# Modulation sums: block transposes and sums by 32 on VectorE ahead of a 128x32 selection matmul, in place of a column sum on TensorE

## The chip, the cores and the metric

One core of one Trainium2 chip. The metric is device time of one execution in microseconds (us); lower is better. The profile is of a single execution, so its own time is given beside the median of the timed runs.

## The reference

Two layers of a decoder trunk on 256 tokens of width 1024, all in float32. Each layer has three sublayers (a SwiGLU feed-forward, a mixer, a SwiGLU feed-forward); the mixer is forgetting attention ("fox") in the first layer and HGRN2 in the second. Around each sublayer stands the same conditioning, from one vector c for the whole sequence:

```python
cond = silu(c)                                              # (1, 1024)
for i in range(2):
    mod = (cond @ ada_w[i] + ada_b[i]).reshape(1, 3, 3, 1, 1024)
    h = rms_norm(x, norm_g[i, s]) * (1 + mod[:, s, 1]) + mod[:, s, 0]
    x = x + gate_factor * mod[:, s, 2] * sublayer(h)        # s = 0, 1, 2
```

So there are 6 sublayers with 3 modulation vectors each (shift, scale, gate), every one of them a product of a 1024-vector with a 1024x1024 matrix `ada_w`. This study is about how the last step of these products is done.

## The kernel before

**The main work.** Activations lie transposed, 128 features by 256 tokens in a tile, 8 tiles. Every weight matrix is streamed from HBM in float32 pieces of 128x1024 (`raw`, 8 buffers). ScalarE rounds a piece to a high part `wh` (line 371), VectorE takes the rest as `wl` (line 372), and TensorE makes each product in three passes (`mm3`, lines 728 to 730): high by high, high by low, low by high. The three buffers of `wh` and `wl` let the split run two weight items ahead of the item that TensorE reads (`SPLIT_AHEAD`). An item of an up-projection is 16 calls of `mm3`.

**The order of the work.** The program is written out as one sequence. `plan` lists the weight items of all sublayers in order and puts the `ada` items (one 128x1024 piece of `ada_w` each) between them, at most of the time of the sublayer before the one that needs them. After each `mm3` the method `tick` counts a clock `now` up by one; it calls `pump`, which emits at most one step of the split (a piece of a main item or one `ada` item), and it advances side tasks. A side task is a generator: it emits some instructions and yields the number of ticks until it is to be advanced again. So one tick is three matmuls of TensorE's queue, and a yield of n puts what follows n `mm3` calls later into the program. A scheduler of the language then sets each engine's instruction order from this sequence and from what is ready in its own model of the time; the engines run their queues in order.

**The modulation, part by part.** For all vectors but the first sublayer's shift and scale, 16 in number (these are called parts here), `ada_step` (line 405) takes the 8 pieces k = 0..7 of the matrix one at a time on VectorE: k = 0 writes `adaacc` = raw times the scalar `cond[:, k]` (line 410), the others add to it (line 412). `adaacc` is 128x1024 and has one buffer: the next part's line 410 must wait until the last reader of the present part is done. After k = 7 the vector is the sum of `adaacc` over its 128 partitions. `ada_finish` (line 459), an urgent side task that is first advanced in the tick of k = 7, makes that sum:

- it waits `SUM_LAG` = 30 ticks;
- line 465: four float32 matmuls, each with a 128x32 block of ones as weights and a strided quarter of `adaacc` (256 columns) as the moving operand. Quarter j writes PSUM partitions 32j to 32j+31, so the four lie in four column groups of the array. All 32 rows of a group hold the same sums. The profile shows each as two records, 8 in all for a part;
- 4 ticks later, line 469: VectorE transposes the 128x256 result in 32x32 blocks from PSUM, which puts the 1024 sums into 8 columns of 128 partitions;
- line 471: VectorE adds the bias `adab`, reading every 32nd column; `set_mods` (line 480) then forms the final vector.

The constants (identity, causal mask, selections) come with one small DMA into `cst` at the start.

Of the kernel before, what the change touches and what calls it, by code (L numbers as in the profile page):

```python
# [11 lines left out]
F32 = mybir.dt.float32  # L12
# [4 lines left out]
ALU = mybir.AluOpType  # L17
AX = mybir.AxisListType

P = 128  # L20
S = 256
D = 1024
# [9 lines left out]

RAW_BUFS = 8
SPLIT_AHEAD = 2
SUM_LAG = 30
FOLD = (5, 4)
H_LAG = 0
HEAD = 7
# [20 lines left out]
def shape_constants():  # L59
    i = np.arange(P)  # L60
    ident = np.eye(P, dtype=np.float32)
    causal = np.where(i[None, :] > i[:, None], np.float32(NEG), np.float32(0)).astype(np.float32)
    lcross = (i[:, None] > i[None, :]).astype(np.float32)
    masks = np.zeros((P, len(LEV), P), np.int32)
    for li, b in enumerate(LEV):
        masks[:, li] = i[:, None] // b == i[None, :] // b
    sel4 = np.zeros((P, 4), np.float32)
    sel1 = np.zeros((P, 1), np.float32)
    for j in range(4):
        sel4[32 * j, j] = 1  # L70
        sel1[32 * j, 0] = 1
    selq = np.zeros((P, 16), np.float32)
    for h in range(16):
        selq[h, h] = -1
        selq[64 + h, h] = -1
    consts = np.concatenate([ident, causal, sel4, selq, sel1], axis=1)
    return (np.ascontiguousarray(consts), np.ascontiguousarray(lcross),
            np.ascontiguousarray(masks.reshape(P, -1)))

# [13 lines left out]
class Trunk:  # L93
# [364 lines left out]

    def ada_finish(self, l, s, part, total):
        nc = self.nc  # L460
        yield SUM_LAG
        ps = self.bank("adaps")
        quarters = total.rearrange("p (c j w) -> p j c w", j=4, w=32)
        for j in range(4):
            nc.tensor.matmul(ps[32 * j:32 * j + 32, :S], self.ones[:, :32], quarters[:, j],  # L465
                             start=True, stop=True, skip_group_check=True)
        yield 4
        tr = self.wk.tile([P, S], F32, tag="adatr", name="adatr", bufs=1)
        nc.vector.transpose(tr, ps[:, :S])
        mod = self.wk.tile([P, 8], F32, tag=f"mod{part}", name=f"mod{l}{s}{part}", bufs=3)  # L470
        nc.vector.tensor_tensor(mod, tr.rearrange("p (c i) -> p c i", i=32)[:, :, 0],
                                self.adab[:, l * 72 + (s * 3 + part) * 8:][:, :8], ALU.add)
        self.set_mods(l, s, part, mod)

    def mod(self, l, s, what):
# [19 lines left out]
    def setup(self):  # L495
        nc, cp, a = self.nc, self.cp, self.a
# [5 lines left out]
        rows = big[:80, 7552:7680]  # L502
        crow = big[:8, 7680:7808]
        self.ident = cp.tile([P, P], F32, name="ident")
        cst = cp.tile([P, 149], F32, name="cst")
        warm = self.w("warm")
        nc.gpsimd.memset(warm[:, 0:1], 0.0)
        nc.scalar.activation(warm[:, 1:2], warm[:, 0:1], AF.Silu)
# [20 lines left out]
            small = small[2:]  # L529
        self.ones = cp.tile([P, P], F32, name="ones")  # L530
        nc.vector.memset(self.ones, 1.0)
        self.sel4 = cst[:, 128:132]
        self.selq = cst[:, 132:148]
        self.sel1 = cst[:, 148:149]
        self.mhalf = cp.tile([P, 2], F32, name="mhalf")
        nc.gpsimd.memset(self.mhalf, -0.5)
        self.tm = cp.tile([P, P], F32R, name="tm")
# [38 lines left out]
        l, s = divmod(self.subs[0], NSUB)  # L576
# [695 lines left out]
def build(inputs, subs=(0, 1, 2, 3, 4, 5), final=True):  # L1272
    nc = bacc.Bacc("TRN2", target_bir_lowering=False, num_devices=1)
    arrays, args = {}, {}
    consts, tmat, lmask = shape_constants()
    every = {n: np.ascontiguousarray(inputs[n]) for n in _INS}
    every["x"] = flip(every["x"])
    every.update(consts=consts, tmat=tmat, lmask=lmask)
    for name, arr in every.items():
        arrays[f"in_{name}_dram"] = arr  # L1280
        args[name] = nc.dram_tensor(f"in_{name}_dram", arr.shape, mybir.dt.from_np(arr.dtype),
                                    kind="ExternalInput").ap()
    out = nc.dram_tensor("out_0_dram", (1, S, D), F32, kind="ExternalOutput").ap()
    with tile.TileContext(nc) as tc:
        with ExitStack() as ctx:
            Trunk(ctx, tc, args, out, list(subs), final).run()
    return nc, arrays
# [6 lines left out]
```

## Time and profile before

| | us |
|---|---|
| median of 3 timed runs | 1105.64 (1105.61 to 1108.42) |
| the profiled execution | 1107.98 |
| its span, first to last instruction | 1106.1 |
| TensorE busy | 1084.1 |
| VectorE busy | 838.7 |
| ScalarE busy | 587.9 |

The mean granted TensorE clock of the profiled execution is 0.995 of full speed. In the profile PE is TensorE's matmul, PEld its weight load, DVE is VectorE, ACT ScalarE, POOL GpSimd, SP SyncE; L465 is line 465 of the kernel. An instruction's recorded duration includes latency that overlaps its neighbour's, so the distance from one start to the next is the better price of one in a full queue. A row of a timeline has start, duration, engine, line, operation, output and inputs, shape and count; the bracket holds the idle time of the engine before it and what ended that.

### The profile page before, as it was taken

Reading aid. Unit: us, or ns where it says so; the run is one execution under the profiler, and the core shown is the slowest. Engines: PE = TensorE matmul, PEld = TensorE weight load, DVE = VectorE, ACT = ScalarE, POOL = GpSimd, SP = SyncE. Lnnn points to the kernel's source line nnn. Section 1 sums busy time; section 2 is a strip of 40 time slices with the busy share of each in tenths; the row PEclk is TensorE's granted clock in tenths of the full one; section 3 lists DMA queues with packets and bytes.
Section 4 is the critical chain, followed back from the end, with each engine's and each line's share of the span. In section 5 each row is a group of like instructions: output and inputs, shape, how many; then the busy total and the mean of one; then the engine's idle time right before and its main releaser. Section 6 shows DMA issues by size and latency. Waiting matters only on the chain.

```text
span 1106.1 us, 22061 instructions
## 1 busy us (share of the span) xinstructions
PE 1084.1 (98%) x8835; PEld 1055.6 (95%) x8835; DVE 838.7 (76%) x1486; ACT 587.9 (53%) x1105; POOL 23.1 (2%) x46
## 2 busy tenths in 40 slices
PE   6999999999999999999999999999999999999997
PEld 6999999988999999999999999999998999999997
DVE  6987789587996797888579888777987879555542
ACT  5454444376865664444355444445777756444443
POOL 0000000020000000000000000000000000000000
PEclk9999999999999999999999999999999999999999
DMA  9999998759974579998958999995643456665530
GB/s 300 334 316 316 323 330 266 213 168 328 298 236 137 162 221 313 312 320 307 259 173 252 286 335 320 322 294 172 191 145 117 122 157 190 188 189 173 179 109 39
DMA packets 304707, 260.24 MB, mean 235 GB/s; under 512 B 9525, under 2 KB 281501, under 8 KB 304605
## 3 DMA queue, kind: packets, MB, share of 16 engines
q1 hardware_dynamic: 304172, 257.79, 76.0%
q8 instruction: 69, 1.13, 0.4%
q0 software_dynamic: 288, 0.52, 0.2%
q10 hardware_dynamic: 144, 0.52, 0.1%
q14 instruction: 34, 0.27, 0.1%
HBM read 257.75 MB, written 1.05 MB: 234 GB/s over the span
## 4 chain that ended last, share of the span: by engine, by line
PE 76%; issue 18%; ACT 3%; POOL 1%; DMA 1%; DVE 1%; SPq 0%; POOLq 0%; DVEq 0%; ACTq 0%
PE pf L729 17%; PE pf L728 16%; PE pf L730 16%; PE pd L728 6%; PE pd L729 6%; PE pd L730 6%; PE pA L1172 1%; ACT wh L371 1%; PE pv L881 1%; PE pv L879 1%; PE pv L880 1%; PE adaps L465 1%; PE sc L998 1%; DMA raw<-in_ffn_w_up_dram 1%; PE pt L1020 1%
## 5 line engine op out<-in xcount | busy, mean ns | idle before, releaser
L729 PE MATMUL pf<-hbuf,wh 128*128 128x256 f32 (+1 forms) x1920 | 543.8, 284 | 0.9 <-DVE hbuf L589 0.9
L730 PE MATMUL pf<-hbuf,wl 128*128 128x256 f32 (+1 forms) x1920 | 543.2, 284 | 0.0
L728 PE MATMUL pf<-hbuf,wh 128*128 128x256 f32 (+1 forms) x1920 | 539.0, 284 | 0.6 <-ACT hbuf L588 0.6
L371 ACT CAST wh<-raw 128x1024 fp32r<-128x1024 f32 x338 | 341.6, 1027 | 370.1 <-PE pf L729 219.0
L372 DVE TENSOR_TENSOR wl<-raw,wh 128x1024 fp32r<-128x1024 f32 x338 | 400.2, 1194 | 158.3 <-ACT wh L371 157.1
L728 PEld LDWEIGHTS pf<-hbuf,wh 128*128 128x128 f32 x1920 | 363.4, 191 | 4.8 <-issue 4.0
L729 PEld LDWEIGHTS pf<-hbuf,wh 128*128 128x128 f32 x1920 | 365.1, 190 | 1.2 <-DVE hbuf L589 1.1
L730 PEld LDWEIGHTS pf<-hbuf,wl 128*128 128x128 f32 x1920 | 364.6, 190 | 0.8 <-issue 0.8
L728 PE MATMUL pd<-gx,wh 128*128 128x256 f32 x704 | 197.5, 281 | 0.0
L729 PE MATMUL pd<-gx,wh 128*128 128x256 f32 x704 | 196.7, 279 | 0.0
L730 PE MATMUL pd<-gx,wl 128*128 128x256 f32 x704 | 196.4, 279 | 0.0
L412 DVE SCALAR_TENSOR_TENSOR adaacc<-raw,cond,adaacc 128x1024 f32<-128x1024 f32 x112 | 142.9, 1276 | 0.9 <-DMA raw<-in_ada_w_dram 0.4
L728 PEld LDWEIGHTS pd<-gx,wh 128*128 128x128 f32 x704 | 132.3, 188 | 2.5 <-issue 2.5
L730 PEld LDWEIGHTS pd<-gx,wl 128*128 128x128 f32 x704 | 132.3, 188 | 0.0
L729 PEld LDWEIGHTS pd<-gx,wh 128*128 128x128 f32 x704 | 132.3, 188 | 0.0
L794 ACT CAST gx<-g 128x256 fp32r<-128x256 f32 x88 | 35.6, 406 | 25.8 <-DVE g L836 18.3
L796 DVE TENSOR_TENSOR gx<-g,gx 128x256 fp32r<-128x256 f32 x88 | 36.6, 418 | 0.2
L410 DVE TENSOR_SCALAR adaacc<-raw,cond 128x1024 f32<-128x1024 f32 x16 | 12.1, 756 | 25.4 <-PE adaps L465 25.4
L836 DVE TENSOR_TENSOR g<-sa,pf 128x256 f32<-128x256 f32 x73 | 30.1, 414 | 0.4 <-ACT sa L835 0.2
L801 DVE SCALAR_TENSOR_TENSOR x<-pd,mod,x 128x256 f32<-128x256 f32 x32 | 14.3, 479 | 20.5 <-PE pd L730 20.5
L835 ACT ACTIVATE sa<-pf 128x256 f32<-128x256 f32 x73 | 27.4, 377 | 0.0
L360 ACT CAST wh<-raw 128x896 fp32r<-128x896 f32 x16 | 15.0, 935 | 23.0 <-DMA raw<-in_ffn_w_up_dram 23.0
(218 smaller groups left out, 859.2 us busy)
## 6 DMA issues: line engine op xcount, KB each, us to landing
raw<-in_ffn_w_up_dram SPq DMA_DIRECT2D x162, 512.0 KB, 5.5
raw<-in_ada_w_dram SPq DMA_DIRECT2D x128, 512.0 KB, 5.8
raw<-in_ffn_w_down_dram SPq DMA_DIRECT2D x76, 512.0 KB, 5.7
raw<-in_fox_w_in_dram SPq DMA_DIRECT2D x32, 512.0 KB, 5.3
raw<-in_hgrn_w_in_dram SPq DMA_DIRECT2D x32, 512.0 KB, 4.5
raw<-in_ada_w_dram SPq DMA_DIRECT2D x32, 256.0 KB, 6.9
raw<-in_ffn_w_up_dram SPq DMA_DIRECT2D x16, 448.0 KB, 6.6
raw<-in_fox_w_out_dram SPq DMA_DIRECT2D x8, 512.0 KB, 5.1
```

Source lines behind the costliest of these rows:

```text
L360: nc.scalar.copy(wh[:, k, cs], raw)
L371: nc.scalar.copy(wh[:, ks, cs], raw)
L372: nc.vector.tensor_tensor(wl[:, ks, cs], raw, wh[:, ks, cs].bitcast(F32), ALU.subtract)
L412: nc.vector.scalar_tensor_tensor(self.ada_acc, raw, self.cond[:, k:k + 1], self.ada_acc, ALU.mult, ALU.add)
L728: nc.tensor.matmul(ps, wh, hx[:, :n], start=first, stop=False, skip_group_check=True)
L729: nc.tensor.matmul(ps, wh, hx[:, lo:lo + n], start=False, stop=False, skip_group_check=True)
L730: nc.tensor.matmul(ps, wl, hx[:, :n], start=False, stop=last, skip_group_check=True)
L794: nc.scalar.copy(dst[:, :S], v)
L796: nc.vector.tensor_tensor(dst[:, lo:lo + S], v, dst[:, :S].bitcast(F32), ALU.subtract)
L801: nc.vector.scalar_tensor_tensor(self.x[:, m, :], ps, gate[:, m:m + 1], self.x[:, m, :], ALU.mult, ALU.add)
L835: nc.scalar.activation(sa, ps[0], AF.Silu)
L836: nc.vector.tensor_tensor(g, sa, ps[1], ALU.mult)
```

## The change

The sum over partitions is split. First VectorE transposes `adaacc` in 32x32 blocks, four chunks of 256 columns, and sums each group of 32 columns of the transposed chunk; the result `red` is 128x32 and holds, at partition 32a+i and column b, the sum of the 32 values of `adaacc` in partitions 32a to 32a+31 at column 32b+i. What is left is to add the four partitions i, 32+i, 64+i, 96+i. TensorE does this with a 128x32 selection matrix `sel32` as weights and 8 columns of `red` as moving operand, four times, into the same four groups of PSUM partitions. The result is in its final place, so the transpose from PSUM falls away and the bias add reads PSUM.

```diff
-SUM_LAG = 30
+SUM_LAG = 8
...
+    sel32 = (i[:, None] % 32 == np.arange(32)[None, :]).astype(np.float32)
...
     def ada_finish(self, l, s, part, total):
         nc = self.nc
+        red = self.wk.tile([P, 32], F32, tag="adared", name="adared", bufs=1)
+        for o in range(0, D, S):
+            tr = self.wk.tile([P, S], F32, tag="adatr", name="adatr", bufs=1)
+            nc.vector.transpose(tr, total[:, o:o + S])
+            nc.vector.tensor_reduce(red[:, o // 32:(o + S) // 32], tr.rearrange("p (b j) -> p b j", j=32), AX.X, ALU.add)
+            yield 3
         yield SUM_LAG
         ps = self.bank("adaps")
-        quarters = total.rearrange("p (c j w) -> p j c w", j=4, w=32)
+        quarters = red.rearrange("p (c j) -> p j c", j=4)
         for j in range(4):
-            nc.tensor.matmul(ps[32 * j:32 * j + 32, :S], self.ones[:, :32], quarters[:, j],
+            nc.tensor.matmul(ps[32 * j:32 * j + 32, :8], self.sel32, quarters[:, j],
                              start=True, stop=True, skip_group_check=True)
         yield 4
-        tr = self.wk.tile([P, S], F32, tag="adatr", name="adatr", bufs=1)
-        nc.vector.transpose(tr, ps[:, :S])
         mod = self.wk.tile([P, 8], F32, tag=f"mod{part}", name=f"mod{l}{s}{part}", bufs=3)
-        nc.vector.tensor_tensor(mod, tr.rearrange("p (c i) -> p c i", i=32)[:, :, 0],
-                                self.adab[:, l * 72 + (s * 3 + part) * 8:][:, :8], ALU.add)
+        nc.vector.tensor_tensor(mod, ps[:, :8], self.adab[:, l * 72 + (s * 3 + part) * 8:][:, :8], ALU.add)
         self.set_mods(l, s, part, mod)
...
-        cst = cp.tile([P, 149], F32, name="cst")
+        cst = cp.tile([P, 176], F32, name="cst")
```

The matmuls of a part thus come 4 x 3 + 8 = 20 ticks after k = 7 instead of 30. Two unused selection constants are dropped, and `cst` grows from 149 to 176 columns.

More of the change, by code (lines that the diff above doesn't have):

```diff
@@ L66, in shape_constants @@
         masks[:, li] = i[:, None] // b == i[None, :] // b
[L67 to L71, printed above, removed]
+    sel32 = (i[:, None] % 32 == np.arange(32)[None, :]).astype(np.float32)
     selq = np.zeros((P, 16), np.float32)
@@ L75, in shape_constants @@
         selq[64 + h, h] = -1
-    consts = np.concatenate([ident, causal, sel4, selq, sel1], axis=1)
+    consts = np.concatenate([ident, causal, selq, sel32], axis=1)
     return (np.ascontiguousarray(consts), np.ascontiguousarray(lcross),
@@ L531, in setup @@
         nc.vector.memset(self.ones, 1.0)
-        self.sel4 = cst[:, 128:132]
-        self.selq = cst[:, 132:148]
-        self.sel1 = cst[:, 148:149]
+        self.selq = cst[:, 128:144]
+        self.sel32 = cst[:, 144:176]
         self.mhalf = cp.tile([P, 2], F32, name="mhalf")
```

## The prediction

> **What bounds the kernel now.** I read the page first: busy shares and the chain that ended last.
>
> ```profile
> span 1106.1 us, 22061 instructions
> PE 1084.1 (98%) x8835; PEld 1055.6 (95%) x8835; DVE 838.7 (76%) x1486; ACT 587.9 (53%) x1105; POOL 23.1 (2%) x46
> ...
> PE pf L729 17%; PE pf L728 16%; PE pf L730 16%; PE pd L728 6%; PE pd L729 6%; PE pd L730 6%; PE pA L1172 1%; ACT wh L371 1%; PE pv L881 1%; PE pv L879 1%; PE pv L880 1%; PE adaps L465 1%; PE sc L998 1%; DMA raw<-in_ffn_w_up_dram 1%; PE pt L1020 1%
> ```
>
> TensorE is busy for 98% of the span, and the chain is made of its matmuls. The step that the change rewrites, L465, is in that chain with about 1%. A busy PE needn't be a full one, so I looked at what TensorE waited for:
>
> ```profile
> PE pv L546 <- DMA ident<-in_consts_dram: 3.2, 1, 3.2
> PE pr L563 <- DMA cst<-in_consts_dram: 2.8, 1, 2.8
> PE rb L688 <- DVE diag L687: 1.8, 3, 1.2
> ```
>
> The columns are total, times, longest. The longest waits are once each, at the start; behind it no wait of its matmuls costs more than 2 us in all. So TensorE's queue is the clock of this kernel: a microsecond taken out of that queue comes off the time, as long as no other engine is late for it. The two questions are how long the 16 sums occupy TensorE, and whether VectorE keeps up.
>
> **TensorE's part.** The timeline of TensorE around the first sum, then its weight loads in the same stretch:
>
> ```profile
> 105.33 0.27 PE L728 MATMUL pf<-hbuf,wh 128*128 128x256 f32 x1
> 105.44 0.28 PE L729 MATMUL pf<-hbuf,wh 128*128 128x256 f32 x1
> 105.56 0.28 PE L730 MATMUL pf<-hbuf,wl 128*128 128x256 f32 x1
> 105.77 0.64 PE L465 MATMUL adaps<-adaacc,ones 128*32 128x256 f32 x8
> 106.34 0.38 PE L728 MATMUL pf<-hbuf,wh 128*128 128x256 f32 x1
> 106.56 0.28 PE L729 MATMUL pf<-hbuf,wh 128*128 128x256 f32 x1
> 106.68 0.29 PE L730 MATMUL pf<-hbuf,wl 128*128 128x256 f32 x1
> ```
>
> ```profile
> 105.45 0.19 PEld L730 LDWEIGHTS pf<-hbuf,wl 128*128 128x128 f32 x1
> 105.77 0.16 PEld L465 LDWEIGHTS adaps<-adaacc,ones 128*32 128x32 f32 x8
> 106.34 0.19 PEld L728 LDWEIGHTS pf<-hbuf,wh 128*128 128x128 f32 x1 [0.41 <-issue]
> ```
>
> Ordinary matmuls start every 0.12 us. Around the sum the starts are 0.21, 0.57 and 0.22 us apart; two ordinary steps would have taken 0.24 of these 1.00 us, so one part takes 0.76 us out of the stream, and 16 parts take 12.2 us: the whole prize if the sum cost TensorE nothing.
>
> The 0.57 us are streaming, and that goes. The rows of this tile give the duration of one record and the count:
>
> ```profile
> L465 PEld LDWEIGHTS adaps<-adaacc,ones x128: 106/108/110, 105.8 to 736.6; 128*32 128x32 f32 x128
> L465 PE MATMUL adaps<-adaacc,ones x128: 379/391/404, 105.8 to 736.8; 128*32 128x256 f32 x128
> L469 DVE STREAM_TRANSPOSE adatr<-adaps x16: 440/443/450, 107.2 to 738.2; 128x256 f32<-128x256 f32 x16
> ...
>   DVE adaacc L410: 25.4, 11
> ```
>
> 128 records are 8 for each of 16 parts. Eight records of 391 ns within 640 ns are two waves of four, one record for each column group; the second wave starts about 0.64 - 0.38 = 0.26 us in. With 8 columns instead of 256 the streaming is next to nothing, and what is left is the fixed price of eight small float32 matmuls. The trace of before has no matmul with 32 columns of weights and few moving columns. Two rows bound it. From above, the sums of the first sublayer, with one moving column but weights of 128 columns:
>
> ```profile
> 28.86 0.95 PE L448 MATMUL adac<-ones,adc 128*128 128x1 f32 x8
> 29.67 0.37 PE L728 MATMUL pf<-hbuf,wh 128*128 128x256 f32 x1
> ```
>
> Eight of them hold the queue for 0.81 us, 0.10 each, although they stream nothing: their weight loads set the pace. At that price a part would be 0.24 us dearer than now, +3.8 us for 16. From below: the eight loads of 128x32 in L465 last 108 ns each and all eight fit into 0.16 us, so they start some 7 ns apart; at that pace eight small matmuls take 0.06 us, and with another 0.1 us until the next ordinary load (an estimate by the first step, which is 0.21 - 0.12 = 0.09 too long) they leave 0.16 of the 0.57 us: 0.41 x 16 = 6.6 us saved. I take the loads as proportional to their columns: 0.10 us / 4 = 0.025 us each, 0.20 us for eight. It lies near the lower row because the change keeps exactly that 128x32 load. So 0.57 becomes 0.20 us, and 16 x 0.37 = 5.9 us leave TensorE's queue.
>
> The 0.09 us by which the first step is over 0.12 us, and the 0.10 us of the last, I leave in place: the new matmuls are 32 columns wide too. If they went, 16 x 0.19 = 3.0 us more would be saved; that is outside my range. The Trainium skill has a rule for it (TensorEngine Tiling (Array Packing), Key Properties): changing the tiling mode drains TensorE. The trace agrees, as the steps into and out of the 32-wide matmuls are 0.21 and 0.22 us long, and by the rule 3.0 us stay.
>
> **VectorE's part.** Added for each part are four block transposes of 128x256 and four sums of 128x256; removed is one transpose. The nearest row of a sum is the maximum over 256 columns, beside an elementwise product of that size:
>
> ```profile
> L1004 DVE TENSOR_REDUCE nm<-sc 128x1 f32<-128x256 f32 x16 | 6.6, 414 | 0.0
> L836 DVE TENSOR_TENSOR g<-sa,pf 128x256 f32<-128x256 f32 x73 | 30.1, 414 | 0.4 <-ACT sa L835 0.2
> ```
>
> By recorded durations 4 x 443 + 4 x 414 - 443 = 2.99 us for a part, 48 us in all. Now the timeline of VectorE from k = 7 of the first part to the start of the next part:
>
> ```profile
> 93.39 1.28 DVE L412 SCALAR_TENSOR_TENSOR adaacc<-raw,cond,adaacc 128x1024 f32<-128x1024 f32 x1
> 95.86 1.23 DVE L372 TENSOR_TENSOR wl<-raw,wh 128x1024 fp32r<-128x1024 f32 x1 [1.19 <-ACT wh L371]
> 97.00 0.41 DVE L836 TENSOR_TENSOR g<-sa,pf 128x256 f32<-128x256 f32 x1
> 97.34 1.22 DVE L372 TENSOR_TENSOR wl<-raw,wh 128x1024 fp32r<-128x1024 f32 x1
> 98.47 0.42 DVE L796 TENSOR_TENSOR gx<-g,gx 128x256 fp32r<-128x256 f32 x1
> 101.56 1.23 DVE L372 TENSOR_TENSOR wl<-raw,wh 128x1024 fp32r<-128x1024 f32 x1 [2.67 <-ACT wh L371]
> ...
> 103.03 1.22 DVE L372 TENSOR_TENSOR wl<-raw,wh 128x1024 fp32r<-128x1024 f32 x1
> 104.16 0.42 DVE L796 TENSOR_TENSOR gx<-g,gx 128x256 fp32r<-128x256 f32 x1
> 106.48 0.75 DVE L410 TENSOR_SCALAR adaacc<-raw,cond 128x1024 f32<-128x1024 f32 x1 [1.90 <-PE adaps L465]
> 107.15 0.44 DVE L469 STREAM_TRANSPOSE adatr<-adaps 128x256 f32<-128x256 f32 x1
> 107.52 1.24 DVE L412 SCALAR_TENSOR_TENSOR adaacc<-raw,cond,adaacc 128x1024 f32<-128x1024 f32 x1
> ```
>
> By starts a transpose takes 0.37 us (107.15 to 107.52) and a 256-column operation 0.34 (97.00 to 97.34), so the eight take 2.8 us, net 2.5 us a part, 39 us in all. Against that stands the wait of L410 for L465, 25.4 us over 11 parts: `adaacc` is now free as soon as VectorE itself has read it. Where the new work goes is seen above: k = 7 ends at 94.67, then VectorE idles 1.19 us, later 2.67 and 1.90 us. 5.8 us of holes hold 2.8 us of work.
>
> Does this make `wl` late? ScalarE's splits show the beat of the main items:
>
> ```profile
> 94.78 1.05 ACT L371 CAST wh<-raw 128x1024 fp32r<-128x1024 f32 x1 [3.12 <-PE pf L729]
> 100.47 1.05 ACT L371 CAST wh<-raw 128x1024 fp32r<-128x1024 f32 x1 [2.61 <-PE pf L729]
> ```
>
> One item takes 5.7 us, and an item is split two items ahead. The split that begins at 100.47 has its second `wl` done at 104.2; TensorE needs it at 100.5 + 11.4 = 111.9. Some 7.6 us of lead cover a burst of 2.8 us. Were that lead gone, each part would cost TensorE up to 2.5 us. ScalarE, the DMA queue on SP and POOL get no new instruction; the earlier freedom of `adaacc` frees `raw` buffers earlier, so loads start no later. The 27 extra columns of `cst` go with a transfer that is there already; I price them at nothing. So I do the bias add of 8 columns, which only reads another place, and the one buffer of `red`: TensorE has read it 20 ticks behind k = 7, and the next part needs it some 30 us later.
>
> Does the new wait bite? TensorE's L465 now waits for the last sum. At 0.36 us a tick (three starts 0.12 apart) the matmuls stood 30 ticks or 10.7 us behind k = 7 in the program, and now 20 ticks or 7.2 us. k = 7 ended 11.1 us ahead of L465, so VectorE is 0.4 us early and has until 94.67 + 7.6 = 102.3. If only one pair (0.7 us) fits into the first hole and the other three (2.1 us) stand behind L796, the last sum is done at 98.8 + 2.1 = 100.9. That leaves 1.4 us. Behind a late sum stand all main matmuls.
>
> The tightest stretch is the attention stage, with three of the 16 sums. Its windows, beside one of a feed-forward:
>
> ```profile
> 276.00:305.00 29.00, 28.92 (x230) 26.57 (x226) 26.51 (x55) 23.17 (x63) 0.00 (x0) 1.00 0.88 289
> 305.00:339.00 34.00, 33.93 (x272) 30.01 (x271) 29.85 (x57) 23.27 (x60) 0.00 (x0) 1.00 0.78 247
> 621.00:651.00 30.00, 30.00 (x261) 29.12 (x259) 24.48 (x31) 13.95 (x21) 0.00 (x0) 1.00 0.97 292
> ```
>
> The third busy column is VectorE. With 2.5 us more the feed-forward window is at 27.0 of 30, the first attention window at 29.0 of 29. There the queue will be full and some of attention's own steps late; I allow 0.5 us of loss, from nothing to 2.5 us for each of the three, 7.5 us.
>
> **Sum.** 5.9 us saved, 0.5 lost: 5.4 us. The profiled execution took 1107.98 us (its span and 1.9 us around it), so it would take 1102.6; it lay 2.3 us above the median of the three timed runs, so against 1105.64 the forecast is 1100.2.
>
> **Rivals.**
>
> *The sum is late for TensorE (slower).* If one more `wl` of the next item comes ahead of the last pair, with its wait for ScalarE, the last sum ends at 101.56 + 1.15 + 0.7 = 103.4 instead of 100.9, 1.1 us after TensorE needs it. In all 16 parts that is 17.6 - 5.9 = 11.7 us slower, 1117.3; it decides once the average lateness is over 0.37 us. For it: the cover shrinks by a third. Against: all four pairs are written within 9 ticks of k = 7, in the first part ahead of the next item's split, and need nothing but VectorE. Chance 0.07.
>
> *The weight loads set the price (slower).* At L448's 0.81 us: +3.8 us, 1109.4. Against: 32-column loads are seen 7 ns apart. Chance 0.04.
>
> *VectorE is full in attention (no change).* If the three parts there cost 2 us each, 6 us eat the gain: 1105.7. The Trainium skill speaks against the change here (VectorE: DVE Perf Modes, Rules for kernel authors): it calls tensor_reduce the slowest operation of that engine and advises restructuring on a hot path. At this size the trace doesn't agree, 414 ns against 414 for a product, so I don't raise the chance: 0.15, along with smaller losses elsewhere.
>
> **The numbers.** The forecast case has 0.74. 0.3% (3.3 us) is about what a measurement of this kernel can tell from no change. Faster by more has the forecast case's 0.74; within it the third rival and half of the weight-load one, 0.17; slower the rest, 0.09. The forecast's own ends are 1099.0 (6.6 saved, none lost) and 1102.3. The range of 8 in 10 goes a little beneath the first, for the 3.0 us of drain, and above to 1104.5, most of the third rival.
>
> **What would show it.** Right: L465 x8 followed by the next L728 after about 0.2 us instead of 0.57; no wait of L410 for L465; VectorE busy some 39 us more; no new wait of L465 for the sum; the windows of the feed-forward shorter by 0.37 us for each sum. Wrong: L465 still above 0.4 us, a wait PE adaps <- DVE adared of more than a few tenths each, or idle time ahead of attention's matmuls.

## The result, and the profile after

| | before | after |
|---|---|---|
| median of the timed runs, us | 1105.79 | 1097.39 |
| their range, us | 1104.51 to 1108.42 | 1097.2 to 1099.45 |
| profiled execution, us | 1107.98 | 1097.96 |
| its span, us | 1106.1 | 1096.2 |

The ratio is 0.9923, with a 95% interval of 0.9911 to 0.9935: 8.4 us faster. The prediction was 1100.2, and its range began a little beneath 1099.0. The direction was right; the time lies under the range, 1.6 us below that 1099.0 and 2.8 us under the forecast.

The page after, first the span and the busy times, then the two new groups of VectorE:

```profile
span 1096.2 us, 22151 instructions
...
PE 1072.4 (98%) x8835; PEld 1049.2 (96%) x8835; DVE 883.3 (81%) x1598; ACT 586.7 (54%) x1105; POOL 23.1 (2%) x46
...
L460 DVE STREAM_TRANSPOSE adatr<-adaacc 128x256 f32<-128x256 f32 x64 | 28.3, 442 | 1.4
L461 DVE TENSOR_REDUCE adared<-adatr 128x8 f32<-128x256 f32 x64 | 26.7, 418 | 1.6
```

TensorE is still busy for 98% and is 11.7 us shorter in busy time; VectorE has 44.6 us more. The timeline of TensorE around the first sum, as the prediction showed it for before:

```profile
99.84 0.28 PE L727 MATMUL pf<-hbuf,wh 128*128 128x256 f32 x1
99.96 0.28 PE L728 MATMUL pf<-hbuf,wl 128*128 128x256 f32 x1
100.17 0.25 PE L467 MATMUL adaps<-adared,cst 128*32 128x8 f32 x8
100.35 0.38 PE L726 MATMUL pf<-hbuf,wh 128*128 128x256 f32 x1
100.57 0.28 PE L727 MATMUL pf<-hbuf,wh 128*128 128x256 f32 x1
```

The starts around the sum are 0.21, 0.18 and 0.22 us apart, 0.61 where two ordinary steps take 0.24. A part takes 0.37 us out of the stream instead of 0.76. The first and the last step are as they were; the middle one fell from 0.57 to 0.18 us.

The waits that bear on the change (total, times, longest, in us), those of VectorE and then those of TensorE:

```profile
DVE adaacc L408 <- DMA raw<-in_ada_w_dram: 16.5, 17, 3.5
...
PE pd L728 <- DVE wl L368: 1.1, 2, 0.7
...
PE adaps L467 <- DVE adared L461: 0.2, 1, 0.2
```

The wait of the first `adaacc` step for the sum, 25.4 us before, is gone. VectorE now runs ahead until it meets the loads of `ada_w` instead (16.5 us). The new wait of the sum for VectorE's last step is there once, 0.2 us. The wait of a main matmul for `wl` lies in the second down-projection: there VectorE stands in `adaacc` behind a load, with a `wl` queued behind it.

**Where the time went in the two traces.** I added up, over all of TensorE's matmuls, by how much each step from one start to the next is longer than 119.3 ns, the mean step of the up-projections in the trace of before. The spans differ by 9.9 us. The sums give 6.1 of it (16 parts: 12.1 us of excess before, 6.0 after). 2.9 us lie in two stretches in which before was at half clock and after wasn't; they are taken up in the last section. The second down-projection lost 1.7 us to the waits above (0.5 in a second profile of the changed kernel). What was not on the list of the prediction is a closer spacing of the ordinary matmuls in the first and the fourth down-projection, 1.7 and 1.0 us. A stretch of 20 us of the first down-projection, free of sums, shows it. The first column after the stretch and its length is PE, busy time and number of matmuls; the number includes two or three that straddle the edges. Before:

```profile
171.00:191.00 20.00, 20.00 (x174) 20.00 (x173) 19.96 (x25) 9.54 (x13) 0.00 (x0) 1.00 0.90 286
```

After:

```profile
168.00:188.00 20.00, 20.00 (x179) 20.00 (x178) 19.45 (x28) 10.11 (x14) 0.00 (x0) 1.00 1.06 322
```

TensorE is busy all of the time at full clock in both, waits for nothing, and still passes five matmuls more. From their starts the step is 116.7 ns before and 113.3 after. The busy share can't show this.

### The profile page after: what moved, and what is told of

Read it like the earlier page. It is cut to its first block, busy times and chain, and to the rows that moved or that the text cites. A ratio compares the mean times of both kernels' runs of the same rounds, so it can differ in the third digit from the quotient of the medians.

```text
span 1096.2 us, 22151 instructions
## 1 busy us (share of the span) xinstructions
PE 1072.4 (98%) x8835; PEld 1049.2 (96%) x8835; DVE 883.3 (81%) x1598; ACT 586.7 (54%) x1105; POOL 23.1 (2%) x46
## 4 chain that ended last, share of the span: by engine, by line
PE 62%; issue 19%; DVE 9%; DMA 5%; ACT 3%; POOL 1%; SPq 0%; POOLq 0%; DVEq 0%; ACTq 0%
PE pf L727 13%; PE pf L726 13%; PE pf L728 13%; PE pd L726 5%; PE pd L728 5%; PE pd L727 5%; DMA raw<-in_ada_w_dram 5%; DVE wl L368 3%; DVE adaacc L408 2%; ACT wh L367 1%; PE pA L1170 1%; PE pv L879 1%; PE pv L877 1%; PE pv L878 1%; PE sc L996 1%
## 5 line engine op out<-in xcount | busy, mean ns | idle before, releaser
L408 DVE SCALAR_TENSOR_TENSOR adaacc<-raw,cond,adaacc 128x1024 f32<-128x1024 f32 x112 | 143.4, 1280 | 17.5 <-DMA raw<-in_ada_w_dram 16.5
L460 DVE STREAM_TRANSPOSE adatr<-adaacc 128x256 f32<-128x256 f32 x64 | 28.3, 442 | 1.4
L461 DVE TENSOR_REDUCE adared<-adatr 128x8 f32<-128x256 f32 x64 | 26.7, 418 | 1.6
```

Of the source, the lines that this page charges most:

```text
L408: nc.vector.scalar_tensor_tensor(self.ada_acc, raw, self.cond[:, k:k + 1], self.ada_acc, ALU.mult, ALU.add)
L460: nc.vector.transpose(tr, total[:, o:o + S])
L461: nc.vector.tensor_reduce(red[:, o // 32:(o + S) // 32], tr.rearrange("p (b j) -> p b j", j=32), AX.X, ALU.add)
```

## The experiments

The theory on entering them: the sums' occupancy of TensorE is the gain, and VectorE's work is hidden. The rivals: the earlier place of the sum or the free `adaacc` brings the gain; VectorE's work costs something; and, later, something other than the sum sets the spacing.

### Is it the earlier sum, or VectorE's work?

**before_lag8** puts the old sum at 8 ticks instead of 30:

```diff
-SUM_LAG = 30
+SUM_LAG = 8
```

> The kernel before with SUM_LAG 8 in place of 30 and nothing else. The sum still streams 256 columns; adaacc comes free 22 ticks (7.9 us) earlier, so VectorE's wait of L410 for L465 (25.4 us over 11 parts) should be all but gone. Theory A (only TensorE's shorter sum pays, 16 x 0.37 us; the rest of the measured 8.4 us is chance of the clock): no change, within 1 us of before. Theory B (the early release of adaacc lets loads and VectorE run ahead and is worth the 2 to 3 us that the sum doesn't explain): 2 to 3 us faster than before.

1103.93 us against 1106.38, ratio 0.9979 (0.9971 to 0.9988). The gain is 2.4 us, and the trace has the larger part of it, 1.7 us, in the attention stage. **before_lag8_att** sets the 8 ticks for the three parts that are summed there and for no other:

```diff
-        yield SUM_LAG
+        yield 8 if (l, s) == (0, 2) else SUM_LAG
```

> The kernel before with a lag of 8 ticks for the three parts that are summed in the attention stage, and 30 for the other thirteen. With 8 everywhere the kernel before gained 2.45 us, and its trace put 2.4 us of that in the attention stage, where TensorE's queue changes less often between kinds of matmul. If the gain is that order: 1.5 to 2.5 us faster than before, with VectorE's wait of L410 for L465 still at some 23 us. If it is the early release of adaacc in the feed-forward stages that lets VectorE and the loads run ahead: less than 0.7 us.

1103.6 against 1106.79, ratio 0.9968 (0.9955 to 0.998): all of it, with three parts. And it is not the early release of `adaacc`, since the wait for it is nearly as long as before, now 24.0 us over 10 parts:

```profile
DVE adaacc L410 <- PE adaps L465: 24.0, 10, 3.2
```

What is left is the order in which the attention stage's matmuls were written out, which differs; no run shows this cause by itself. That gain is not part of the change: the projection matmuls of that stretch (numbers 1800 to 2400) take 102.39 us before, 100.60 here and 101.44 after, and the changed kernel's three cheaper sums alone make up the last difference (1.0 us).

**after_lag18** puts the changed kernel's sums at 30 ticks again:

```diff
-SUM_LAG = 8
+SUM_LAG = 18
```

> The changed kernel with SUM_LAG 18 in place of 8, so that TensorE's matmuls stand 30 ticks behind k = 7 as before the change, and not 20. Theory A and B: the same as the changed kernel within 0.7 us (1097.4), at most a few tenths faster where TensorE waited for the last sum. Theory C (the earlier modulations themselves pay): 2 us or more slower than the changed kernel.

1097.48 us, ratio 0.9922 (0.9909 to 0.9935): the same as the change. The earlier place brings nothing.

**before_dve** adds VectorE's transposes and sums to the kernel before and leaves their result unused:

```diff
-        yield SUM_LAG
+        red = self.wk.tile([P, 32], F32, tag="adared", name="adared", bufs=1)
+        for o in range(0, D, S):
+            tr = self.wk.tile([P, S], F32, tag="adatr", name="adatr", bufs=1)
+            nc.vector.transpose(tr, total[:, o:o + S])
+            nc.vector.tensor_reduce(red[:, o // 32:(o + S) // 32], tr.rearrange("p (b j) -> p b j", j=32), AX.X, ALU.add)
+            yield 3
+        yield SUM_LAG - 12
```

> The kernel before with the four block transposes and four sums by 32 of each part added on VectorE, their result unused, and TensorE's sum as before at the same 30 ticks. It prices VectorE's added work alone (39 us by starts). Theory A: hidden but for 0.5 to 2 us, so 0.5 to 2 us slower than before. Rival (VectorE near full in the attention stage): 4 us or more slower. If VectorE's work is wholly hidden: within 0.3 us of before.

1106.78 us, ratio 1.0003 (0.9992 to 1.0014). VectorE's 64 pairs are hidden where nobody waits for their result.

### What do the matmuls cost, and when is the sum late?

**after_nomm** leaves out the four matmuls, and with them the adding of the four groups of partitions; the bias add reads `red`.

```diff
-        for j in range(4):
-            nc.tensor.matmul(ps[32 * j:32 * j + 32, :8], self.sel32, quarters[:, j],
-                             start=True, stop=True, skip_group_check=True)
...
-        nc.vector.tensor_tensor(mod, ps[:, :8], self.adab[:, l * 72 + (s * 3 + part) * 8:][:, :8], ALU.add)
+        nc.vector.tensor_tensor(mod, red[:, :8], self.adab[:, l * 72 + (s * 3 + part) * 8:][:, :8], ALU.add)
```

> The changed kernel without the four matmuls of a part: the bias is added to the first 8 columns of VectorE's partial sums, so the adding of the four groups of partitions is left out. In the changed kernel's trace the 16 parts still take 5.6 to 5.9 us out of TensorE's stream. Theory A (that is a serial price): 5 to 6 us faster than the changed kernel, 1091.5 to 1092.5. Rival (the step is hidden in the queue and its price is an artefact of modelled ends): less than 2 us faster.

1091.07 us, ratio 0.9864 (0.9843 to 0.9885), 6.3 us under the change. The trace of the change has 6.0 us in its sums. So what TensorE's queue loses to a sum is on the path. That it is so in full is only near: in the trace of after_nomm the second down-projection is also 1.1 us shorter for its spacing and waits, which are no part of the sums.

**after_dve2** does VectorE's transposes and sums twice over:

```diff
+            tr = self.wk.tile([P, S], F32, tag="adatr", name="adatr", bufs=1)
+            nc.vector.transpose(tr, total[:, o:o + S])
+            nc.vector.tensor_reduce(red[:, o // 32:(o + S) // 32], tr.rearrange("p (b j) -> p b j", j=32), AX.X, ALU.add)
```

> The changed kernel with the block transposes and sums of each part done twice (the second writes the same values): some 59 us more on VectorE at the 0.93 us that a pair takes in the changed kernel's trace, nothing else. Theory A (VectorE's work is hidden but for places where TensorE already waits for wl): 1 to 4 us slower than the changed kernel. Rival (VectorE is near its limit and sets the pace in the stages with modulation loads): 10 us or more slower. Wholly hidden: within 0.7 us.

1109.73 us, ratio 1.0026 (1.0012 to 1.0041), 12.3 us above the change: my own theory's 1 to 4 us fell. TensorE's waits for the sum:

```profile
PE adaps L470 <- DVE adared L464: 12.1, 10, 4.1
```

Eight pairs of 0.93 us (below) are 7.4 us, and the cover is 20 ticks, 7.2 us. So a late sum costs what the first rival said, as soon as the work exceeds the cover.

**after_lag0** takes 8 of the 20 ticks away instead:

```diff
-SUM_LAG = 8
+SUM_LAG = 0
```

> The changed kernel with SUM_LAG 0, so that TensorE's matmuls stand 12 ticks (4.3 us) behind k = 7 in place of 20. Four pairs of transpose and sum take 3.7 us by the changed kernel's trace, and two splits stand among them. It prices the rival of the prediction, a sum that comes late for TensorE. Rival right about the mechanism: a wait of L467 for adared in most parts, 0.5 to 1.5 us each, 5 to 20 us slower than the changed kernel. If VectorE runs far enough ahead: within 1 us of it.

1102.55 us, ratio 0.9958 (0.9943 to 0.9974), 5.2 us above the change. The waits for the sum are smaller than the loss:

```profile
PE adaps L467 <- DVE adared L461: 2.7, 6, 1.1
```

The sums' excess on TensorE rose by 3.3 us (9.3 against 6.0). The rest, 1.9 us, I can't place in one profile, which also has a stretch at half clock (62.56 to 65.97 us) that the change's profile has not. The cover of 12 ticks is too short, and that of 20 is enough.

### How small can TensorE's part be?

**sel128** replaces the four 32-wide matmuls by one at full width: a 128x128 selection, `red` with all its 32 columns as moving operand, and the choice of the right quarter in the bias add (four small adds on VectorE).

```diff
-        for j in range(4):
-            nc.tensor.matmul(ps[32 * j:32 * j + 32, :8], self.sel32, quarters[:, j],
-                             start=True, stop=True, skip_group_check=True)
+        nc.tensor.matmul(ps[:, :32], self.sel32, red, start=True, stop=True, skip_group_check=True)
...
+        for j in range(4):
+            q = slice(32 * j, 32 * j + 32)
+            nc.vector.tensor_tensor(mod[q], sums[q, j], bias[q], ALU.add)
```

> The changed kernel with one matmul of a 128x128 selection matrix (ones where row and column agree modulo 32) by the 128x32 partial sums, in place of four 32-column matmuls; VectorE then picks the right column of each of the four groups of 32 partitions with four small adds instead of one (about 0.5 us more on VectorE for a part). In the changed kernel's trace a part still takes about 0.39 us out of TensorE's stream. Theory A with the steps into and out of the 32-column groups as the price (0.1 us each): the part costs 0.15 to 0.25 us, 2 to 4 us faster than the changed kernel, 1093.5 to 1095.5. Rival (the step is the price of any float32 matmul in this stream, not of the groups): within 1 us of the changed kernel.

1093.91 us, ratio 0.9886 (0.9873 to 0.9898). Run again:

> The full-width selection matmul again, beside the version with half as many chunks and on the same chip: 1093 to 1095 us, about 3.5 us under the changed kernel, if its first four runs were typical; a trace that shows whether the 113.3 ns spacing in the third feed-forward's down-projection comes back.

1093.29 us, ratio 0.9876 (0.9859 to 0.9893). TensorE's timeline around the first sum in this second run:

```profile
100.70 0.28 PE L729 MATMUL pf<-hbuf,wl 128*128 128x256 f32 x1
100.82 0.30 PE L465 MATMUL adaps<-adared,cst 128*128 128x32 f32 x2
100.96 0.36 PE L727 MATMUL pf<-hbuf,wh 128*128 128x256 f32 x1
101.16 0.28 PE L728 MATMUL pf<-hbuf,wh 128*128 128x256 f32 x1
```

Steps of 0.12, 0.14 and 0.20 us: a part costs 0.22 instead of 0.37 us, 2.1 us less for 16 by the traces (6.0 to 3.9). The step into the sum is an ordinary one now, the step out of it keeps its 0.20. The other 1.4 to 2 us against the change lie in the spacing and in the second down-projection's waits: the third down-projection steps by 113.3 ns and not by 117.8, the fourth by 117.8 and not by 114.8. The second has 116.6 and still 1.3 us of waits in one run, and 113.3 and no wait in the other. I didn't take them apart further.

**sel128_half** is sel128 with two chunks of 512 columns in place of four of 256 (and the causal mask kept in the start buffer to make room):

```diff
-        for o in range(0, D, S):
+        for o in range(0, D, 512):
...
-            yield 3
+            yield 6
```

> The full-width selection matmul, and VectorE's work in two chunks of 512 columns in place of four of 256: two transposes and two sums, fewer pairs that wait for each other (0.93 us a pair now, of which 0.70 are work). About 0.6 us less on VectorE for a part. The causal mask moves into the start buffer to make room. If TensorE's remaining waits for wl (1.1 us in the trace of the full-width kernel) and nothing else hang on VectorE: 0.5 to 1.5 us faster than the full-width kernel's 1093.9. If VectorE's work is hidden: the same within 0.7 us.

1093.67 us, ratio 0.9888 (0.9874 to 0.9903): the same. Fewer instructions on VectorE bring nothing.

### What sets the spacing?

A second profile of each kernel first, unchanged:

> The kernel before again, for its trace. The traces of three kernels with the old sum had two windows of 3.41 us in which TensorE's granted clock was halved, at 61 to 67 us and 228 to 234 us, worth some 1.5 us each, beside the start. If the windows belong to the program, both stand here again; if they are chance of the execution, one or both are missing or stand elsewhere. The same for the spacing of the matmuls: 116.7 ns in the first down-projection, 113.3 ns in the traces with the new sum. If it belongs to the program it is 116.7 ns again.

> The changed kernel again, for its trace. In its first trace no window had a halved clock between the start and the end, and the matmuls of the first down-projection stood 113.3 ns apart. If these belong to the program, both hold again; if they are chance, a window appears near 61 or 228 us, or the spacing is another.

Before: 1108.58 us, and the first down-projection steps by 116.7 ns, as in the first profile. After: 1095.33 us, and 113.4, as in the first profile. So the spacing belongs to the kernel. It isn't quite fixed, though: the second down-projection of the changed kernel has a mean of 117.4 ns in one profile and 114.9 in the other.

**before_break** and **after_break** add one small matmul ahead of each down-projection and one in it, to see if the way into a stretch picks the spacing:

```diff
+            if m in (0, 2):
+                pb = self.bank("brk")
+                nc.tensor.matmul(pb[:, 0:1], self.ident, self.ones[:, 0:1], start=True, stop=True,
+                                 skip_group_check=True)
```

> The kernel before with one small extra matmul (128x128 weights, one moving column, float32, into a spare bank, result unused) ahead of each down-projection and once within it: 8 in all, some 0.2 to 0.3 us each, 2 us. Theory entry: the start-to-start time of the ordinary matmuls is picked by how a stretch is entered; then the steps in some of the four down-projections differ from those of before (113.3, 116.7 or 117.8 ns), and the first lasts other than 63.0 us by 0.7 us or more; the time shifts by 1 to 3 us either way beside the 2 us. Theory layout: the spacing belongs to where the tiles lie in memory; the steps stay at 116.7 ns in the first and fourth down-projection, and the kernel is 2 us slower than before.

> The changed kernel with the same 8 extra matmuls. Theory entry: some of its down-projections leave 113.3 ns, and the first lasts more than 60.5 us by 1 to 3 us. Theory layout: steps of 113.3 ns stay in the first and fourth, and the kernel is 2 us slower than the change, about 1099.4.

**before_layout** gives the kernel before the changed kernel's tiles and leaves its sums alone:

```diff
-        cst = cp.tile([P, 149], F32, name="cst")
+        cst = cp.tile([P, 176], F32, name="cst")
...
+        red = self.wk.tile([P, 32], F32, tag="adared", name="adared", bufs=1)
+        nc.vector.memset(red, 0.0)
```

> The kernel before with the changed kernel's tiles: constants 176 columns wide, and the tile of the sums by 32 allocated and written once for each part by a small VectorE instruction that nobody reads; its own sums stay as they were. Theory layout: the ordinary matmuls step by 113.3 ns in the first and fourth down-projection, these last 60.5 and 62.5 us instead of 63.0 and 63.5, and it is some 2.5 us faster than before, about 1103.2. Theory entry: the stages last as before, 63.0 and 63.5 us, and the time is that of before within 1 us.

The steps in this table and the next are means over the 528 matmuls of a down-projection; steps over 150 ns, at sums, waits and extra matmuls, are left out.

| | us | ratio to before | mean step in the four down-projections, ns |
|---|---|---|---|
| before | 1106.21 | | 116.7, 117.2, 117.2, 116.8 |
| before_break | 1108.72 | 1.0022 (1.0011 to 1.0032) | 117.3, 116.7, 117.1, 116.7 |
| after (its own comparison, above) | 1097.39 | 0.9923 | 113.4, 117.4, 117.8, 114.8 |
| after_break | 1098.08 | 0.9928 (0.9913 to 0.9943) | 116.7, 114.3, 114.5, 113.9 |
| before_layout | 1098.94 | 0.9937 (0.9922 to 0.9952) | 113.4, 113.4, 114.2, 114.8 |

This was the surprise of the study. Wider constants, with the old sum left as it is, make the kernel before 7.3 us faster, three times what I had expected, and almost as fast as the change. The same stretch of before_layout as above:

```profile
170.00:190.00 20.00, 20.00 (x179) 20.00 (x178) 19.96 (x25) 10.18 (x15) 0.00 (x0) 1.00 0.94 291
```

All four down-projections are closer, 6.3 us in all against before by the traces. (The spans of the two profiles differ by 9.8 us: before also has the two stretches at half clock of the last section, and before_layout has neither.) The tiles behind `cst` in memory begin 96 bytes later. The extra matmuls tell the rest: with the old layout no stage comes near 113.3 ns whatever the way in; with the new one the steps are 113.3 or 117.8 by turns, and the break moved which (the first down-projection lost the closer one, the second and third won it). Here is the third down-projection of after_break, ahead of the extra matmul at 706.47 us and behind it:

```profile
699.00:706.40 7.40, 7.40 (x65) 7.40 (x64) 5.38 (x7) 2.00 (x2) 0.00 (x0) 1.00 0.98 340
707.00:714.40 7.40, 7.40 (x67) 7.40 (x67) 7.36 (x11) 4.69 (x8) 0.00 (x0) 1.00 1.01 354
```

The step goes from 117.7 to 113.4 ns there; in the first down-projection the extra matmul at 173.84 us turns 113.6 into 117.8. In the first three down-projections of before, after, before_layout and after_break the step changes at an interruption of the stream alone, a sum, a wait or an extra matmul, and often it doesn't change even there. So in these traces the layout goes with which values there are, and an interruption can pick another of them. Each of the sums is such an interruption.

Which tile? The split weights `wh` and `wl` moved from 32 bytes past a multiple of 64 onto a multiple. **before_w64** and **after_w32** shift them alone, by an unused tile of 32 bytes ahead of them (and one ahead of the work tiles, which thus move by 64):

```diff
+        self.wp.tile([P, 8], F32, tag="spare", name="spare", bufs=1)
+        self.wk.tile([P, 8], F32, tag="spare", name="spare2", bufs=1)
```

> The kernel before with two unused 32-byte tiles, one ahead of the split weights and one ahead of the work tiles: the weights wh and wl move by 32 bytes, from 32 past a multiple of 64 to a multiple of 64, as in the changed kernel; all else stays as it was with respect to 64 bytes, and no instruction is added. Theory weight address: the spacing of the ordinary matmuls goes by where the weights lie; all four down-projections step by 113.3 ns, as with the wider constants, and the time is about 1099 us, 6 to 7 under before. Theory moving operand or constants: some other tile that the wider constants move is the cause; then the steps stay at 116.7 to 117.8 ns and the time at that of before within 1 us.

> The changed kernel with the same two unused tiles: its wh and wl move from a multiple of 64 bytes to 32 past one, where they lay before; the sums by 32 on VectorE stay. Theory weight address: the first and fourth down-projections take 63.0 and 63.5 us as before, and what is left is the change itself: 5.6 us less in the sums, less 0 to 1.7 us of waits in the second down-projection; about 1100.2 us, from 1099.5 to 1101.5, ratio 0.995. Theory moving operand or constants: 1097.4, as the change.

**sel128_pitch** is sel128 with the two halves of `hbuf` 272 columns apart, so that every moving operand of the up-projections begins at a multiple of 64 bytes:

```diff
+HP = 272
...
+        self.hbuf = [cp.tile([P, KC, 2 * HP], F32R, name=f"hbuf{i}") for i in range(2)]
...
+            nc.vector.scalar_tensor_tensor(u[:, HP:HP + S], self.x[:, k, :], gs, u[:, :S].bitcast(F32),
```

> The full-width variant with the two halves of hbuf 272 columns apart instead of 258, so that every moving operand of the up-projections begins at a multiple of 64 bytes (now only every fourth k of the first half does); the transposed chunk goes through the mx tiles to make room. Theory address, for the moving operand too: the ordinary matmuls of the up-projections, some 5700, step by 113 to 117 ns instead of 119.3 on average; 14 to 34 us less than the 1093.5 of the full-width variant, if the loads keep up (their engines are 9 tenths busy in these stages, so less is likelier than more). Theory weights only: the up-projections stay at 119 ns and the time at 1093.5 within 2 us.

| | us | ratio to before | `wh`, bytes past a multiple of 128 | mean step in the four down-projections, ns |
|---|---|---|---|---|
| before | 1106.37 | | 96 | 116.7, 117.2, 117.2, 116.8 |
| before_w64 | 1114.1 | 1.007 (1.0056 to 1.0083) | 0 | 119.9, 120.0, 120.0, 119.9 |
| after_w32 | 1102.9 | 0.9972 (0.9964 to 0.9981) | 96 | 117.9, 118.1, 117.9, 118.3 |
| sel128_pitch | 1093.05 | 0.9886 (0.9873 to 0.99) | 64 | 113.9, 117.8, 113.9, 117.8 |

The theory of 64 bytes fell at once: before_w64, with the weights on a multiple of 64, is 7.7 us slower than before and not 7 us faster. The same stretch there:

```profile
172.00:192.00 20.00, 20.00 (x169) 20.00 (x168) 19.70 (x24) 9.23 (x12) 0.00 (x0) 1.00 0.89 282
```

And in after_w32:

```profile
170.00:190.00 20.00, 20.00 (x171) 20.00 (x170) 18.39 (x26) 9.09 (x13) 0.00 (x0) 1.00 1.06 318
```

169 matmuls in 20 us, 174, or 179, by 32 bytes here and there: shown is that the layout alone does it, in both directions, and that a 32-byte spare tile ahead of the weights and one ahead of the work tiles are enough. The remainder past 128 bytes (the last table; before_layout, after and sel128 have 64) orders the three values in all these kernels, but that is a fit made afterwards, and 96 has two sets of values, so no rule is shown. Nor is it shown whether the weights or the work tiles matter; the moving operand `gx` of the down-projections lies at one place in all of them, so of what TensorE reads there only `wh` and `wl` moved. With the moving operand on 64 bytes the four up-projections step by 118.7, 118.9, 118.9 and 119.0 ns (118.7, 119.0, 119.1 and 119.9 in sel128's second run), and the time is that of sel128: no gain from that.

## Why the prediction was wrong in its size

**TensorE's part: right.** Eight small matmuls with their drain were put at 0.20 us where the long ones took 0.57; it is 0.18. The saving of 5.9 us is 6.1 in the traces, and after_nomm, 6.3 us faster without the 6.0 us that were left, shows that such a term is on the path. The price taken, a quarter of a full-width load, lay where the nearest row pointed; L448's price (the second rival) did not come. The steps of 0.21 and 0.22 us stayed in place, and with them the 3.0 us. The rule of the Trainium skill on a change of tiling mode (TensorEngine Tiling (Array Packing), Key Properties) covers only half of this: in sel128, at full width, the entry step is gone, the exit step of 0.20 us isn't.

**VectorE's part: hidden as said, with two sizes off.** A pair was put at 0.70 us by starts of independent neighbours. A transpose and the sum that reads it wait for each other, as VectorE's timeline shows, here the end of the first part and the beginning of a later one:

```profile
98.90 0.42 DVE L461 TENSOR_REDUCE adared<-adatr 128x8 f32<-128x256 f32 x1
...
514.92 0.45 DVE L460 STREAM_TRANSPOSE adatr<-adaacc 128x256 f32<-128x256 f32 x1
515.40 0.42 DVE L461 TENSOR_REDUCE adared<-adatr 128x8 f32<-128x256 f32 x1
515.85 0.45 DVE L460 STREAM_TRANSPOSE adatr<-adaacc 128x256 f32<-128x256 f32 x1
```

A pair takes 0.93 us. A part with four is 3.7 us instead of 2.8. In the first part the last sum ended at 98.90 + 0.42 = 99.32, 0.85 us before TensorE began at 100.17; the lead was put at 1.4 us. The loss was placed in the attention stage and put at 0.5 us; that stage lost nothing that can be seen (102.39 us before and 101.44 after, above), and the second down-projection lost 0.5 to 1.7. The reason given against a loss, that `adaacc` frees `raw` earlier so loads start no later, isn't contradicted by the traces, but VectorE then catches up with the loads and waits in its queue ahead of `wl`. The third rival named the wrong place; its price did not come.

**The first rival: right in its mechanism, not in this kernel.** The wait for the sum is 0.2 us in all. With a cover of 12 ticks, or with twice the work, it comes: 5.2 and 12.3 us.

**The step that failed: "The 27 extra columns of `cst` go with a transfer that is there already; I price them at nothing."** The transfer costs nothing. The place of everything behind `cst` in memory does: the same columns take 7.3 us off the kernel before, and its traces show 6.3 us of closer spacing. In the changed kernel two of the four down-projections got the closer spacing, and 2.2 us of its gain over all stages are that. The **Sum**, 5.4, therefore lacked a term of some 2 us. With 6.1 for the sums, 2.2 for the spacing and 0.5 to 1.7 lost, 6.6 to 7.8 of the measured 8.4 us (7.2 to 9.8 by the interval) are accounted for; the rest is within what the half-clock stretches can do. The range could not hold it, since its lower end had only the drain below the forecast.

That leaves the question how much the change is worth by itself, and the runs give two answers. With the new layout, before_layout is the kernel to compare with, since its tiles lie where the changed kernel's do: 1098.94 us against 1097.39, ratios of 0.9937 and 0.9923 with intervals that overlap. That is 1.5 us, not clear of the noise. The spans of the two profiles are 1096.3 and 1096.2 us. The sums take 6.1 us less in the changed kernel; the second down-projection has 1.7 us of waits; and the second and third step by 117.4 and 117.8 ns where before_layout has 113.4 and 114.2, 4.0 us more. So between these two profiles nearly all of what the sums save is lost again, most of it by the other spacing. How much is lost isn't fixed: in the second profile of the changed kernel the second down-projection steps by 114.9 ns with 0.5 us of waits, and the span is 1093.6 us.

With the old layout only a correction can tell. after_w32, with its weights back at the old remainder, is 3.1 us faster than before by the ratio; but its spacing is 3.0 us worse than before's over all stages, so this isn't the old layout either. Corrected for that it is 6.1 us, near the 5.4 of the forecast. This correction is worked out from one profile, not measured.

## What to carry to other kernels

When TensorE's queue is the clock, price a small matmul by the distance of the starts around it, and check that the work ahead of it fits into the cover. A tile that changes its size moves all tiles behind it: before crediting an edit with a gain of a few tenths of a per cent, run the old kernel with the new layout and compare with that, and try a spare tile or two for its own sake. For this kernel the full-width selection is the best version found (1093.3 to 1093.9 us), 1.1 to 1.2% under before.

## What the runs showed of the hardware

**The spacing goes by the layout.** Ordinary 128x256 matmuls, all with TensorE busy and at full clock, step by 113.3, 116.7, 117.8 or 120.0 ns (117.3 or 118.7 in after_w32), steadily from one interruption of the stream to the next, often for 20 us and more, in kernels that differ by where tiles lie. Over the some two thousand steps of the four down-projections, 3 ns a step are 6 us. The Trainium skill (SBUF — State Buffer, Operand start alignment) has a rule for where an operand may start, says that it is about legality and not speed, and that its runs timed nothing; these runs show that the place of the tiles has a price, from 0.7% more (before_w64) to 0.6% less (before_layout) of the time here.

**Half-clock stretches of 3.41 us.** In the profile of before, the window list gives two, one of them this (the third number from the end is the granted clock):

```profile
61.25:64.66 3.41, 3.41 (x17) 3.41 (x17) 3.40 (x6) 1.23 (x2) 1.10 (x2) 0.50 1.09 328
```

17 matmuls where 28 fit at 0.12 us. The other begins at 228.50. Neither profile of the changed kernel has one there; before_lag8_att, whose program is that of before up to there, has neither. The Trainium skill (TensorE: Matmul & The Clock Gate, Part 1: The HAM clock gate) describes a free-running window of 3413 ns and half rate after an idle one; the length and the 0.50 agree. The stretch just ahead of this one, 57.84 to 61.25 us, was not idle, though: TensorE was busy for 2.55 of its 3.41 us. The stretches don't belong to the old sum either: after_lag0 and after_w32 have one each, at 62.56 and 60.98 us. So one and the same work can run with such stretches or without, 2.9 us in the excess of this profile, and no pair of profiles should be read closer than that.
